# Five input tiles in flight, the first two convolutions cut by token group, the norm row spread by TensorE, and the first prefix recurrence moved from slot 2 to slot 3: one change to a hybrid decoder layer

## The chip, the cores and the metric

The kernel runs on the 8 cores of one Trainium2 chip. The time is the device time of the slowest core in microseconds (us). Where it matters, ratios are given to the kernel before that ran on the same chip in the same rounds. Some executions fall into a second, slower state, in which the cores of one die show a lower granted TensorE clock (one run of the kernel before took 2349.65 us); those are left out everywhere.

Engines are named as the profile names them: PE is TensorE (PEld its weight loads), DVE VectorE, ACT ScalarE, POOL GpSimd, SP SyncE.

## The reference

One step of a hybrid decoder layer, for four prompts of 2048 tokens and 128 sample sequences of 8 tokens. Cut to what the change touches:

```python
D_MODEL = 2048; C_A = C_B = 1024; CONF_KW = 31; LRU_KW = 4; D_FF = 6144

def mixer(xn, conf_buf, lru_buf, h0, p, reset_first):
    proj = xn @ p['w_in']
    a_val, a_gate, b_x, b_gate = jnp.split(proj, [C_A, 2 * C_A, 2 * C_A + C_B], axis=-1)
    u = a_val * jax.nn.sigmoid(a_gate)
    ca, new_conf = causal_dwconv(u, conf_buf, p['conf_dw_w'], p['conf_dw_b'])      # 31 taps
    ca = jax.nn.silu(layer_norm(ca, p['conf_ln_g'], p['conf_ln_b']))
    xc, new_lru = causal_dwconv(b_x, lru_buf, p['lru_conv_w'], p['lru_conv_b'])    # 4 taps
    h, h_last = rglru(xc, h0, ...)      # two 128x128 gate products per head, sigmoids, a scan over time
    cb = h.astype(xn.dtype) * jax.nn.gelu(b_gate)
    return jnp.concatenate([ca, cb], axis=-1) @ p['w_out'], new_conf, new_lru, h_last

# layer:  x + norm(mixer(norm(x)));  then  x + norm(conv_ffn(norm(x)))   -- the larger part of the time
```

A core takes half of one prompt's tokens (1184 "active" columns with its samples) and, because the recurrence runs over time, a prefix of 992 columns for which only the recurrence is computed. That makes 17 tiles of 128 tokens. Tiles 0 to 9 in loading order carry the active columns, tiles 10 to 16 the rest of the prefix.

## The kernel before

The program is written once as a list of operations with the buffers that each reads and writes. Each engine executes its own operations in exactly the order in which they stand in the program; semaphores are derived from the buffers. So where a line stands decides what it queues behind on its engine. `mm` goes to PE, `act` to ACT, `tt`, `ts`, `stt` and `dcopy` to DVE.

A tile is loaded, normed (a square with sum on ACT, a 128x2048 scaling on DVE) and turned (16 transposes on PE into two PSUM banks, each evacuated by one copy on DVE or ACT):

```python
def p0_load(n):
    i, sl = xorder[n], n % 3                                # three tile buffers
    load("sp", r_x, T[f"xt{sl}"][:], xall[128 * i:128 * i + 128, :], [], [(f"xt{sl}",)])

def p0_norm(n):
    ...
    act(xs[:], xt[:], AF.Square, [kx], [ks, ("tiny", sl, 0)], accum=c[:, 0:1])
    act(c[:, 1:2], c[:, 0:1], AF.Ln, ...)
    act(c[:, 2:3], c[:, 1:2], AF.Exp, ...)
    stt(xs[:], xt[:], c[:, 2:3], T["grow0"][:], ALU.mult, ALU.mult, [kx, ("tiny", sl, 2), "grow0"], [ks])

def p0_turn(n):
    for kh in range(2):
        ...                                                 # 8 transposes of 128x128 into bank 6 + kh
        eng = "act" if kh == 1 and n % 2 == 0 else "dve"
        evac(eng, ...)                                      # PSUM -> xna (active) or xnp (prefix)
```

The first stage projects channel groups 0 and 1 for five groups of tokens, while the tiles come in. `conv_diag(j)` builds the 31 diagonal matrices with which a depthwise convolution runs on PE; it is one DVE instruction.

```python
p0_load(0)
setup_first()            # vectors, flags, identity; the norm row broadcast by DMA to 128 partitions
p0_load(1)
load_w(2, after=[("xt0",)])
p0_load(2)
load_w(4, after=[("xt2",)])
conv_diag(0)
p0_norm(0)
G5 = [(0, 160), (160, 416), (416, 672), (672, 928), (928, NACT)]
def early(g):            # gate and value projection of channel groups 0 and 1, one token group
    ...
p0_norm(1); setup_second(); conv_diag(1); conv_load(0); conv_load(1)
for g in range(5):
    n = 2 * g
    p0_load(n + 3); p0_turn(n)
    p0_load(n + 4); p0_turn(n + 1)
    p0_norm(n + 2)
    if g < 4: p0_norm(n + 3)
    early(g)
...
b = conv(0, range(5), turn_more)    # turn_more: one of the tiles 10 to 16 between the pieces
conv_out(0, b)
b = conv(1, range(5), turn_more)
P_bx(0)                             # prefix projection of recurrence 0
conv_out(1, b); P_evac(0); P_conv(0)
```

After that come slots 2 to 7, each with one channel group of the convolution module and parts of one recurrence:

```python
for j in range(2, 8):
    i = j - 1
    ...
    proj(bg, "g", j, ACT3);  act(T["th"][:], ..., AF.Sigmoid, ...)
    if j == 2: P_gate(0, "wab"); P_sig(0, "p1", V_BA)
    else:      P_gate(i - 1, "wxb"); P_sig(i - 1, "p3", V_BX); P_in(i - 1); P_mult(i - 1)
    proj(bv, "v", j, ACT3);  uout(j, ...)
    if j == 2: P_gate(0, "wxb"); P_sig(0, "p3", V_BX); P_in(0); P_mult(0)
    P_scan(i - 1)                   # DVE scan over time
    P_bx(i)                         # prefix projection (PE)
    P_evac(i)                       # PSUM -> SBUF (ACT)
    P_conv(i)                       # four-tap convolution and cast to bf16 (DVE)
    bc = conv(j, [0])
    P_gate(i, "wab")
    conv_out(j, bc)
    P_sig(i, "p1", V_BA)
```

Of the kernel before, what the change touches and what calls it, by code (L numbers as in the profile page):

```python
# [55 lines left out]
class Sched:  # L56
# [135 lines left out]
    "hm23": 0, "gbg2": 0, "xna1": 4640, "x2_0": 0, "ca1": 0, "xnp1": 23584, "dstg": 2304, "ca2": 39456, "wp3": 8448,  # L192
    "t1_1": 23584, "wp7": 12544, "A3": 44096, "xcpZ": 48736, "diag0": 48736, "xs2_1": 16640, "xn21": 20736, "hstf":
    52704, "wo00": 39200, "catA5": 47392, "diag1": 56672, "xnp0": 64608, "hm3": 16640, "hm4": 39200, "t2_0": 28512,
    "wu2": 80480, "wo10": 8192, "xna0": 84576, "xn20": 49728, "wo13": 68192, "grow3": 18944, "t2_1": 33440, "wu4":
    103520, "xs1": 39456, "wu1": 107616, "ca4": 111712, "ca6": 116352, "ca7": 120992, "hm11": 41504, "ca5": 125632,
    "catB6": 76384, "f34": 2304, "ge1": 43808, "xc1": 53248, "wo01": 125632, "og0": 68192, "grow1": 78720, "bxp":
    130272, "ov0": 72928, "f31": 27136, "ca0": 134272, "catA7": 103520, "p3Z": 53248, "hm1": 77664, "hm14": 79968,
    "hm12": 82272, "t3_1": 58176, "hm13": 84576, "grow2": 86912, "x2_1": 95104, "t3_0": 63104, "wu3": 138912,
    "wo02": 105856, "hP": 143008, "bxe": 68032, "catA4": 133824, "ssf": 33280, "fl": 33568, "wo12": 114048, "grow0":  # L200
    111712, "rs": 72992, "hm7": 86880, "wp11": 103296, "t1_0": 143040, "f30": 43808, "f36": 49952, "wp5": 107392,
    "ubf1": 143040, "wab": 147968, "xsh": 122240, "hm0": 89184, "catA2": 136160, "wxb": 150016, "ov1": 111488,
    "us1": 146368, "cv": 152064, "vecs": 152192, "ge0": 116224, "hm5": 91488, "hm6": 93792, "xcb1": 49728, "flags":
    155072, "tiny": 155104, "gh": 138496, "xcb0": 77632, "dj": 37664, "btl": 155360, "f37": 56096, "bxpZ": 57216,
    "hm18": 96096, "p1Z": 143040, "ffo": 120992, "f32": 62240, "xs2": 119904, "hh1": 68384, "catB7": 123264,
    "identb": 155456, "catB3": 155712, "catA0": 158048, "ht": 143040, "gbg1": 160384, "ffp": 48576, "hm17": 98400,
    "slruc": 165024, "slruh": 166560, "xcp": 155712, "wp4": 133280, "f33": 111488, "xt1": 124000, "xcpbZ": 61216,
    "xs2_0": 165024, "hh0": 117632, "wo11": 169120, "wp1": 160384, "hm15": 100704, "hm20": 137376, "sq": 159680,
    "f38": 125824, "catA1": 177312, "wo03": 179648, "hm21": 139680, "catB2": 187840, "hm10": 141984, "lrucf":
    190176, "xc0": 167072, "wp6": 155712, "gbg0": 191808, "hm19": 144288, "wu0": 172000, "xt2": 176096, "hm22":  # L210
    146592, "hm16": 148896, "catB0": 196448, "p1": 176096, "hh2": 164480, "A3b": 184288, "ve1": 169120, "f35":
    172672, "wp8": 178816, "p3": 180064, "us0": 147008, "th": 167072, "mu": 179648, "catB4": 198784, "catA6":
    201120, "wu5": 198784, "hm9": 182912, "catB5": 203456, "ubf0": 188928, "hm2": 185216, "wp0": 190176, "hm8":
    187520, "xh": 205792, "prv": 194272, "zh": 194272, "xs0": 192256, "wp2": 200416, "wp9": 204512, "ve0": 173888,
    "ones": 164416, "ca3": 202880, "xcpb": 192256, "catB1": 207840, "catA3": 210176, "wp10": 208608, "xt0": 202880,
    "og1": 194272,
# [3 lines left out]
def build_program():  # L220
# [36 lines left out]
    with ExitStack() as es:  # L257
# [17 lines left out]
            ("grow0", [D], F_, 0, 2), ("wab", [8, 128], B_, 1, 18), ("wxb", [8, 128], B_, 1, 18),  # L275
            ("slruc", [8, 16, 3], F_, 1, 18), ("slruh", [8, 16], F_, 1, 18),
# [4 lines left out]
            ("bxp", [3 + NPRE], F_, 2, 9), ("xcp", [NPRE], F_, 2, 9), ("xcpb", [NPRE], B_, 2, 9),  # L281
            ("p1", [NPRE], F_, 2, 9), ("p3", [NPRE], F_, 2, 9),
# [13 lines left out]
        for i in range(3):  # L296
            BUFS += [(f"gbg{i}", [NCAT], F_, (9.5, 10, 11)[i], (18, 18.4, 17)[i])]
            BUFS += [(f"xt{i}", [D], F_, 0, 2), (f"xs{i}", [D], B_, 0, 2)]
            BUFS += [(f"hh{i}", [D], F_, 22.9, 24)]
# [17 lines left out]
        for i in range(8):  # L317
            BUFS += [(f"ca{i}", [NCAT], F_, max(1, i), (11, 13, 15, 17)[i // 2])]
# [82 lines left out]
        seq += [("g", 0), ("v", 0), ("g", 1), ("v", 1), ("x", 0)]  # L401
        for j in range(2, 8):
            seq += [("g", j), ("v", j), ("x", j - 1)]
# [25 lines left out]
        def setup_first():  # L429
            load("sp", r_su, vecs[:], vecs_d, [], ["vecs"])  # L430
            load("sp", r_su, flags[:], flags_d, [], ["flags"])
            load("pool", r_su, identb[:], ident_d, [], ["identb"])
            load("sp", r_su, T["grow0"][:], grows_d[0:1, :].partition_broadcast(128), [], ["grow0"])

        def setup_second():
            act(cv[:, 0:8], vecs[:, V_LAM:V_LAM + 8], AF.Exp, ["vecs"], [("cv", "e")], scale=-1.0)
            act(cv[:, 0:8], cv[:, 0:8], AF.Ln, [("cv", "e")], [("cv", "l")], bias=1.0)
            ts(cv[:, 8:16], cv[:, 0:8], -4.0, None, ALU.mult, None, [("cv", "l")], [("cv", "h")])
            ts(cv[:, 0:8], cv[:, 0:8], -8.0, None, ALU.mult, None, [("cv", "l")], [("cv", "f")])
            ts(cv[:, 16:32], vecs[:, V_BA:V_BA + 16], 0.5, None, ALU.mult, None, ["vecs"], [("cv", "b")])  # L440
            memset(ones[:], 1.0, [], ["ones"])
# [4 lines left out]
        def p0_load(n):  # L446
            i, sl = xorder[n], n % 3
            load("sp", r_x, T[f"xt{sl}"][:], xall[128 * i:128 * i + 128, :], [], [(f"xt{sl}",)])

        def p0_norm(n):  # L450
            sl = n % 3
            xt, xs, kx, ks = T[f"xt{sl}"], T[f"xs{sl}"], (f"xt{sl}",), (f"xs{sl}",)
# [4 lines left out]
            stt(xs[:], xt[:], c[:, 2:3], T["grow0"][:], ALU.mult, ALU.mult, [kx, ("tiny", sl, 2), "grow0"], [ks])  # L457

        def p0_turn(n):
            i, sl = xorder[n], n % 3  # L460
            xs, ks = T[f"xs{sl}"], (f"xs{sl}",)
            for kh in range(2):
# [9 lines left out]
                eng = "act" if kh == 1 and n % 2 == 0 else "dve"  # L472
# [55 lines left out]
        def conv(j, tags, between=None):  # L528
# [4 lines left out]
            for g in range(4):  # L533
# [8 lines left out]
                if between is not None:  # L542
                    between(g)
            return b0

        def conv_out(j, b0):
# [5 lines left out]
            kk = [(kc, 0), (kc, 1)]  # L552
            if j == 0:
                dcopy(T["A3b"][:], ca[:], kk, ["A3b"])
                act(T["A3"][:], ca[:], AF.Square, kk, ["A3"])
            else:
                sq = T["sq"][:, 0:NCAT]
                act(sq, ca[:], AF.Square, kk, ["sq"] + [("sq", g) for g in range(5)])
                tt(T["A3b"][:], T["A3b"][:], ca[:], ALU.add, kk + ["A3b"], ["A3b"])
                tt(T["A3"][:], T["A3"][:], sq, ALU.add, ["sq", "A3"], ["A3"])  # L560
# [17 lines left out]
        def pb(j, name):  # L578
            return name + ("Z" if j == 7 else "")

        def P_evac(j, b0=6):
            nb = pb(j, "bxp")
            bxp = T[nb]
            if j == 0 or j == 7:
# [178 lines left out]


        p0_load(0)
        setup_first()
        p0_load(1)
        load_w(2, after=[("xt0",)])
        p0_load(2)
        load_w(4, after=[("xt2",)])  # L770
        conv_diag(0)
        p0_norm(0)
        G5 = [(0, 160), (160, 416), (416, 672), (672, 928), (928, NACT)]
        stb = {"b": 0}

        def early(g):
            a0, a1 = G5[g]
            n = a1 - a0
            for j in range(2):
                gt, kg = (T["th"], ("th", g)) if j == 0 else (T["sq"], ("sq", g))  # L780
                bs = []
                for kind in "gv":
                    b = stb["b"] % 6
                    stb["b"] += 1
# [6 lines left out]
                act(gt[:, a0:a1], pg, AF.Exp, PK(bs[0]), [kg], scale=-1.0)  # L791
                act(gt[:, a0:a1], gt[:, a0:a1], AF.Ln, [kg], [kg], bias=1.0)
                act(gt[:, a0:a1], gt[:, a0:a1], AF.Exp, [kg], [kg], scale=-1.0)
                uout(j, pv, gt[:, a0:a1], PK(bs[1]) + [kg], a0, a1, g)

        p0_norm(1)
        setup_second()
        conv_diag(1)
        conv_load(0)
        conv_load(1)  # L800
        for g in range(5):
            n = 2 * g
            p0_load(n + 3)
            p0_turn(n)
            p0_load(n + 4)
            p0_turn(n + 1)
            p0_norm(n + 2)
            if g < 4:
                p0_norm(n + 3)
            early(g)  # L810
        done_w("v", 1)

        nx = {"n": 10}

        def turn_more(g):
            n = nx["n"]
            if n >= 17:
                return
            if n + 3 < 17:
                p0_load(n + 3)  # L820
            if n + 1 < 17:
                p0_norm(n + 1)
            p0_turn(n)
            nx["n"] += 1

        trip["n"] = 0
        b = conv(0, range(5), turn_more)
        conv_out(0, b)
        b = conv(1, range(5), turn_more)
        P_bx(0)  # L830
        conv_out(1, b)
# [4 lines left out]

        for j in range(2, 8):
            conv_load(j)
            i = j - 1
# [560 lines left out]
```

## Time and profile before

| | before |
|---|---|
| median | 1879.52 us (1877.62, 1879.52 and 1879.96) |
| profiled execution, slowest core (3) | 1875.9 us |
| first transposes / first projection / second token group start | 17.65 / 32.62 / 49.50 us |
| convolution 2 ends | 186.2 us |
| gate product after convolution 4 | 263.84 us |
| first output-projection matmul, cores 0 to 7 | 552, 558, 549, 559, 556, 548, 557, 549 us |

The page of the profile of before, its top, its rows of PE and of PE's granted clock in 40 slices of 47 us, and the summary of the chain of waits:

```profile
span 1875.9 us, 33549 instructions; the slowest of 8 cores (1863.6 to 1875.9 us)
...
PE 1757.1 (94%) x10400; PEld 913.3 (49%) x10400; DVE 988.9 (53%) x994; ACT 564.0 (30%) x1007; POOL 126.9 (7%) x239
...
PE   2889999989987999999999999999999999999993
...
PEclk9999999989988999999999999999999999999997
...
PE 85%; DMA 8%; ACT 2%; DVE 2%; issue 2%; SPq 0%; POOL 0%; DVEq 0%; ACTq 0%; POOLq 0%
```

PE is busy 94% of the time and 85% of the chain is PE itself. What an off-path engine does is free here, except where PE waits for it. The first digit of the PE row is a 2: in the first 47 us PE works two tenths of the time. That slice is the change's target.

The timeline of core 3 before (start in us, length, engine, line, operation, out<-in, shape, count, and in brackets the idle time before it with what ended it):

```profile
10.84 4.29 DVE L359 TENSOR_TENSOR sb_diag_102<-sb_identb,sb_vecs 128x3968 bf16<-128x3968 bf16 x1 [10.84 <-DMA sb_identb<-ident]
15.05 2.34 DVE L368 SCALAR_TENSOR_TENSOR sb_xs_92<-sb_xt_91,sb_tiny,sb_grow_51 128x2048 bf16<-128x2048 f32 x1
17.65 1.87 PE L467 MATMUL ps<-sb_identb,sb_xs_92 128*128 128x128 bf16 x16 [17.65 <-DVE sb_xs_92 L368]
...
26.84 0.53 POOL L377 DMA_DIRECT2D sb_wu_187<-w_in  x1 [17.31 <-DMA sb_xt_99<-xall]
...
32.62 1.22 PE L374 MATMUL ps<-sb_xna_130,sb_wu_185 128*128 128x160 bf16 x8
...
40.76 1.23 PE L374 MATMUL ps<-sb_xna_130,sb_wu_187 128*128 128x160 bf16 x8 [3.92 <-DMA sb_wu_187<-w_in]
...
49.50 1.03 PE L374 MATMUL ps<-sb_xna_130,sb_wu_185 128*128 128x256 bf16 x8 [0.19 <-DVE sb_xna_130 L347]
...
186.19 0.58 PE L374 MATMUL ps<-sb_xcpb,sb_wab 128*128 128x496 bf16 x2
...
263.84 0.58 PE L374 MATMUL ps<-sb_xcpb,sb_wab 128*128 128x496 bf16 x2
```

The first tile had landed at 8.0 us, but DVE was building the diagonals of convolution 0 (4.29 us at 10.84), and the tile's scaling stood behind it. The third weight was issued only at 26.84 us, and PE waited 3.92 us for it at 40.76.

The waits of PE on that core in the first 200 us, by releaser (total us, number of waits, longest):

```profile
PE ps L467 <- DVE sb_xs_92 L368: 17.6, 1, 17.6
PE ps L467 <- DVE sb_xna_130 L347: 17.4, 5, 11.2
PE ps L467 <- DVE sb_xnp_131 L347: 5.3, 1, 5.3
PE ps L374 <- DMA sb_wu_187<-w_in: 3.9, 1, 3.9
```

The transposes of a tile wait for the evacuation of the tile before, because both use PSUM banks 6 and 7.

### The profile page before, as it was taken

The page shows a single profiled execution, that of the slowest core. Times are in us where ns is not written, and L with a number is a line of the kernel's source. Part 1 is how long each engine was busy: PE and PEld are TensorE (multiplying, and loading weights), DVE is VectorE, ACT ScalarE, POOL GpSimd, SP SyncE. Part 2 cuts the span into 40 slices and gives each one's busy share as a digit, 9 for nine tenths or more (in the row PEclk, how much of TensorE's full clock was granted, in tenths as well). Part 3 has the DMA queues.
Part 4 walks back from the last instruction along what each step waited for, and adds up shares of the span by engine and source line. Part 5 has one row for each costly group of instructions (what it writes and reads, how often), then busy time and mean ns, then how long its engine had stood idle before and what let it go on. Part 6 is the DMA issues. An engine that isn't in the chain of part 4 may idle for free.

```text
span 1875.9 us, 33549 instructions; the slowest of 8 cores (1863.6 to 1875.9 us)
## 1 busy us (share of the span) xinstructions
PE 1757.1 (94%) x10400; PEld 913.3 (49%) x10400; DVE 988.9 (53%) x994; ACT 564.0 (30%) x1007; POOL 126.9 (7%) x239
## 2 busy tenths in 40 slices
PE   2889999989987999999999999999999999999993
PEld 2765555544442444555555544444555555544441
DVE  4544545547884565666666640002666666652243
ACT  2642343257883443222222211111222222211121
POOL 1000000001120001000000000001000000000000
PEclk9999999989988999999999999999999999999997
DMA  8653233222258547744444325556444444355756
GB/s 202 204 129 64 45 81 53 50 35 46 46 99 206 171 153 158 135 69 68 68 69 68 68 63 118 118 118 124 68 68 69 68 69 69 68 138 116 187 195 199
DMA packets 54259, 194.25 MB, mean 104 GB/s; under 512 B 7232, under 2 KB 10944, under 8 KB 46656
## 3 DMA queue, kind: packets, MB, share of 16 engines
q0 software_dynamic: 29232, 106.41, 33.7%
q1 hardware_dynamic: 24848, 85.69, 13.5%
q8 instruction: 84, 1.38, 0.3%
q14 instruction: 95, 0.78, 0.1%
HBM read 267.56 MB, written 32.35 MB: 160 GB/s over the span
## 4 chain that ended last, share of the span: by engine, by line
PE 85%; DMA 8%; ACT 2%; DVE 2%; issue 2%; SPq 0%; POOL 0%; DVEq 0%; ACTq 0%; POOLq 0%
PE ps L374 85%; DMA sb_xt_99<-xall 2%; DMA sb_wo_206<-w_out 1%; DMA sb_prv<-f_scr 1%; DMA sb_xt_95<-xall 1%; DMA y<-sb_hh_101 1%; DMA sb_wu_187<-w_in 1%; DMA y<-sb_hh_97 1%; ACT L341 0%; PE ps L467 0%; PE ps L1043 0%; DMA sb_wab<-wa 0%; SPq L377 0%; DVE sb_fl L359 0%; DVE sb_ht L368 0%
## 5 line engine op out<-in xcount | busy, mean ns | idle before, releaser
L347 DVE COPY sb_ve_113<-ps 128x1026 f32<-128x1026 f32 (+1 forms) x48 | 36.4, 800 | 297.8 <-PE ps L374 297.8
L347 DVE COPY sb_ve_127<-ps 128x1026 f32<-128x1026 f32 (+1 forms) x48 | 36.4, 800 | 114.1 <-PE ps L374 114.1
L368 DVE SCALAR_TENSOR_TENSOR sb_ov_129<-sb_ve_127,sb_vecs,sb_ov_129 128x1184 f32<-128x1184 f32 x48 | 69.7, 1451 | 5.3 <-DVE sb_ov_129 L368 0.5
L368 DVE SCALAR_TENSOR_TENSOR sb_og_128<-sb_ge_126,sb_vecs,sb_og_128 128x1184 f32<-128x1184 f32 x48 | 69.7, 1452 | 5.0
L368 DVE SCALAR_TENSOR_TENSOR sb_og_114<-sb_ge_112,sb_vecs,sb_og_114 128x1184 f32<-128x1184 f32 x48 | 69.7, 1451 | 5.0
L368 DVE SCALAR_TENSOR_TENSOR sb_ov_115<-sb_ve_113,sb_vecs,sb_ov_115 128x1184 f32<-128x1184 f32 x48 | 69.6, 1451 | 5.0
L339 ACT COPY sb_dstg<-ps 128x512 f32<-128x512 f32 x36 | 20.9, 587 | 159.6 <-PE ps L374 159.6
L374 PE MATMUL ps<-sb_ubf_117,sb_diag_116 128*128 128x342 bf16 (+1 forms) x496 | 64.1, 291 | 0.0
L374 PE MATMUL ps<-sb_ubf_103,sb_diag_102 128*128 128x342 bf16 (+1 forms) x496 | 62.2, 286 | 0.0
L339 ACT COPY sb_ffo<-sb_ve_127 128x32 f32<-128x32 f32 x24 | 5.3, 219 | 182.6 <-DVE sb_ve_127 L347 182.6
L339 ACT COPY sb_ffo<-sb_ve_113 128x32 f32<-128x32 f32 x24 | 5.3, 220 | 175.5 <-DVE sb_ve_113 L347 175.5
L341 ACT ACTIVATE sb_og_128<-sb_og_128 128x1184 f32<-128x1184 f32 x24 | 28.6, 1191 | 83.0 <-DVE sb_og_128 L368 83.0
L374 PEld LDWEIGHTS ps<-sb_ubf_117,sb_diag_116 128*128 128x128 bf16 x496 | 43.9, 99 | 19.7
L341 ACT ACT_TABLE_LOAD x37 | 47.5, 1283 | 17.9 <-PE ps L374 7.0
L341 ACT ACTIVATE sb_og_114<-sb_og_114 128x1184 f32<-128x1184 f32 x24 | 28.6, 1192 | 79.3 <-DVE sb_og_114 L368 79.3
L374 PEld LDWEIGHTS ps<-sb_ubf_103,sb_diag_102 128*128 128x128 bf16 x496 | 43.2, 97 | 18.5
L339 ACT COPY sb_ge_112<-ps 128x1026 f32<-128x1026 f32 (+1 forms) x48 | 31.4, 706 | 33.6 <-PE ps L374 33.6
L339 ACT COPY sb_ge_126<-ps 128x1026 f32<-128x1026 f32 (+1 forms) x48 | 31.4, 706 | 27.4 <-PE ps L374 27.4
L374 PE MATMUL ps<-sb_xna_130,sb_wu_187 128*128 128x512 bf16 (+2 forms) x184 | 34.2, 333 | 3.9 <-DMA sb_wu_187<-w_in 3.9
L374 PE MATMUL ps<-sb_xn_132,sb_wp_207 128*128 128x512 bf16 (+1 forms) x192 | 35.1, 325 | 0.5 <-DVE sb_xn_132 L347 0.5
L374 PE MATMUL ps<-sb_xn_132,sb_wp_209 128*128 128x512 bf16 (+1 forms) x192 | 35.1, 325 | 0.3 <-ACT sb_ge_112 L339 0.3
L374 PE MATMUL ps<-sb_xn_135,sb_wp_207 128*128 128x512 bf16 (+1 forms) x192 | 35.1, 325 | 0.1
(671 smaller groups left out, 4067.5 us busy)
## 6 DMA issues: line engine op xcount, KB each, us to landing
f_scr<-sb_dstg SPq DMA_DIRECT2D x36, 256.0 KB, 3.5
sb_prv<-f_scr SPq DMA_DIRECT2D x36, 256.0 KB, 5.6
sb_xt_91<-xall SPq DMA_DIRECT2D x6, 1024.0 KB, 6.8
sb_xt_95<-xall SPq DMA_DIRECT2D x6, 1024.0 KB, 10.4
sb_xt_99<-xall SPq DMA_DIRECT2D x5, 1024.0 KB, 11.3
sb_x_0_110<-xall SPq DMA_DIRECT2D x5, 1024.0 KB, 6.7
h_scr<-sb_x_0_110 SPq DMA_DIRECT2D x5, 1024.0 KB, 3.8
sb_x_1_124<-xall SPq DMA_DIRECT2D x4, 1024.0 KB, 5.2
```

What stands on the lines that cost most here:

```text
L339: S.op("act", lambda e: e.copy(out=out, in_=in_), reads, writes)
L341: S.op("act", lambda e: e.activation(out=out, in_=in_, func=func, scale=scale, bias=bias), reads, writes)
L347: S.op("dve", lambda e: e.tensor_copy(out, in_), reads, writes)
L368: S.op("dve", lambda e: e.scalar_tensor_tensor(out, a, s, b, op0, op1), reads, writes)
L374: S.op("pe", lambda e: e.matmul(out, lhsT, rhs, start=start, stop=stop, skip_group_check=skip), reads, writes)
```

## The change

Its intent: get the first stage off the ground sooner, and have PE work ready while tiles arrive.

1. Five tile buffers at first instead of three, and all four weights queued as soon as tile 0 has landed.
2. The norm row comes as one row of 8 KB and is spread over the partitions by four one-row matmuls and four copies, instead of a broadcast DMA. Half of the vector table loads later.
3. The diagonal builds move behind the first two token groups, and tile norms and turns move between the projections of a group.
4. Convolutions 0 and 1 run per token group (`early_conv`), and projection 2 and convolution 2 run before the first prefix projection.
5. Recurrence 0 starts in slot 3 instead of slot 2's first gate; slot 3 now holds two recurrences, with a second set of buffers ("Y").

The diff, without the new table of buffer addresses and the smaller edits:

```diff
 def p0_load(n):
-    i, sl = xorder[n], n % 3
+    i, sl = xorder[n], xslot(n)             # n % 5 for the first ten tiles
 def p0_norm(n):
     ...
     stt(xs[:], xt[:], c[:, 2:3], T["grow0"][:], ALU.mult, ALU.mult, ...)
+    if n + XD(n) < 17:
+        p0_load(n + XD(n))
 def p0_turn(n):
-    eng = "act" if kh == 1 and n % 2 == 0 else "dve"
+    eng = "act" if kh == 1 and (n % 2 == 0 or n < 4) else "dve"
 ...
+load("sp", r_su, T["grow0"][0:1, :], grows_d[0:1, :], [], [("grow0r", c) for c in range(4)])
+p0_load(0)
+...
+load_w(4, after=[("xt0",)])
+for n in range(1, 5):
+    p0_load(n)
+for c in range(4):
+    mm(PS[:, 512 * c:512 * c + 512], ones[0:1, :], T["grow0"][0:1, 512 * c:512 * c + 512], True, True, ...)
+for c in range(4):
+    dcopy(T["grow0"][:, 512 * c:512 * c + 512], PS[:, 512 * c:512 * c + 512], ...)
+p0_norm(0); setup_second(); p0_norm(1); conv_load(0); conv_load(1)
+def next_tile(n):
+    if n < 17:
+        p0_turn(n)
+    if n + 2 < 17:
+        p0_norm(n + 2)
+next_tile(0)
+next_tile(1)
 for g in range(5):
-    ...
-    early(g)
+    early(g, lambda j: next_tile(2 * g + 2 + j))    # after the projections of channel group j
+    if g < 2:
+        conv_diag(g)
+    if g >= 2:
+        early_conv(g - 2)
+    ...
+# projection 2 (gate), early_conv(3, [0]), projection 2 (value), early_conv(3, [1]), conv(2), tiles 12 to 16 between
+P_bx(0)
 ...
-for j in range(2, 8):
+for j in range(3, 8):
+    if j == 3:
+        P_bx(1, bx1); P_evac(1, bx1)
     proj(bg, "g", j, ACT3)
     A_gate(j, bg)
+    if j in (3, 4):
+        P_gate(j - 3 + (j == 4), "wab"); P_sig(j - 3 + (j == 4), "p1", V_BA)
+        if j == 3: P_conv(1)
     ...
     proj(bv, "v", j, ACT3)
     uout(j, ...)
+    if j in (3, 4):
+        h = 0 if j == 3 else 2
+        P_gate(h, "wxb"); P_sig(h, "p3", V_BX); P_in(h); P_mult(h); P_scan(h)
+    if j == 3:
+        P_gate(1, "wab"); P_sig(1, "p1", V_BA)
+        bc = conv(j, [0])
+        P_gate(1, "wxb"); P_sig(1, "p3", V_BX)
+        conv_out(j, bc)
+        P_in(1); P_mult(1)
+        P_bx(2)
+        P_evac(2)
+        P_scan(1)
+        P_conv(2)
+        continue
```

## The prediction

> **What bounds the kernel now.** PE is busy 94% of 1875.9 us; the chain of waits is 85% PE. The change touches only the first 190 us. The slice table shows PE at 2 tenths in the first 47 us. The timeline of the slowest core (3):
> - first tile landed at 8.0 us, but its scaling stood behind a 4.3 us diagonal build on DVE; first transposes 17.6 us;
> - tile 0's evacuation stood behind the norm of tile 1 (landed 20.3 us); first projection 32.6 us;
> - projections j=1 waited for weights (40.6, 43.9 us) issued only at 26.8 us, because three tiles, two weights and a 1 MB broadcast of the norm row filled the DMA until 26.3 us;
> - second token group 49.5 us; then waits of 4.8 and 5.3 us for tiles near 57 and 110 us, and 1.3 us each for gate weights (153 us) and a sigmoid (163 us);
> - convolution 2 ended at 186.2 us.
>
> Warm durations: 256-column group 7.0 us, convolution 15.3, tile transpose 0.89, prefix projection 6.7. All PE work up to 186.2 us is 32 + 3x15.3 + 17x0.89 + 2x6.7 + 16 + 1 = about 124 us, so 62 us are lost there.
>
> **What changes.**
> - The broadcast becomes an 8 KB row, four one-row matmuls and four copies, hidden under the first tile's load; half the vector table goes later. About 1.2 MB of early DMA vanish: 4-5 us at the 250-290 GB/s of mixed loads.
> - Five tiles and four weights queue at once; the idle DMA at 26-29 us (windows: 0.00) goes.
> - The diagonal build (4.3 us) and a table load (1.28 us) leave the first tile's path.
> - Convolutions 0 and 1 go per token group, and projection 2 and convolution 2 ahead of the first prefix projection, so PE has work while tiles 10-16 arrive. Matmul columns do not change.
> - New SBUF layout: I found no buffer whose predecessor is freed later in a way that matters; two output-weight loads should go 1 us earlier.
>
> **Estimate.** The first stage stays DMA-bound: 5 tiles, 4 weights and state, about 9.5 MB. Tiles beside weights came at 6.85 us per MB: tiles 1-3 at about 15, 21, 28 us; weights at 132 GB/s from 8.5 us: the last at about 40 us. First projection about 27 us, second token group 43-44 us instead of 49.5. From there PE is nearly always fed: 115 us of work plus 3 us of handoffs ends at about 161 us; the same work (without three gate products) ends at 185 us before. Gain 24 us. Slot 3 now holds two recurrences: 1.5 us lost behind a sigmoid (1.3 us seen at 163 us). Output weights +1. Net 23.5 us; the later stages, PE-bound, keep it.
>
> **Prediction: 1856 us, 8 in 10 between 1844 and 1867.** Faster by over 2%: 0.07; within 2%: 0.92; slower: 0.01.
>
> **The Trainium skill.** "TensorE: Matmul & The Clock Gate", part 1, says that the array runs at half rate after an idle window of about 3.4 us. The trace agrees: 16 transposes took 1.87 us after idle, 1.06 warm. About 2 us of the gain is clock, inside the figure.
>
> **What would show it.** First transposes near 14 us; second group near 43 us; no PE wait over 2 us between 45 and 160 us; prefix projection 1 ends near 161 us; from slot 4 on, every stage as long as before, shifted by 23 us.
>
> **What would make it wrong.** Weights served much later beside five queued tiles (gain 15); PE waiting on ACT in the early groups, since each gate stands behind the norm of a tile that may not have landed; PE stalls in slots 3-4 where recurrences pile up; output weights arriving no earlier, so part of the gain is waited away near 560-600 us.

## The result and the profile after

The median was 1871.47 us (1870.89 to 1873.81), against a median of 1879.52 us for before. The ratio is 0.9962 (95% interval 0.9943 to 0.9982), which counts as the same at the 2% threshold. It is above the predicted range of 1844 to 1867. A ratio here is the record's own figure, from the fast runs of the same rounds, so it is not quite the ratio of the medians.

The page after, the same lines:

```profile
span 1869.5 us, 33611 instructions; the slowest of 8 cores (1861.7 to 1869.5 us)
...
PE 1751.6 (94%) x10302; PEld 916.9 (49%) x10470; DVE 988.8 (53%) x997; ACT 569.0 (30%) x1016; POOL 128.5 (7%) x239
...
PE   6899899989987999999999999999999999999992
...
PEclk9899999999997999999999999999999999999996
...
PE 84%; DMA 7%; DVE 3%; ACT 3%; issue 2%; SPq 0%; POOL 0%; DVEq 0%; ACTq 0%; POOLq 0%
```

The first slice went from 2 tenths to 6: the target was hit. But the second slice of the clock row (47 to 94 us) fell from 9 to 8, the fifth of the PE row (187 to 234 us) fell from 9 to 8 too, and the second of the PE row is still 8. So something new is lost in both places. DVE and ACT grew from 2% to 3% of the chain.

The timeline of core 4 (the slowest after) in the first stage:

```profile
14.25 1.87 PE L474 MATMUL ps<-sb_identb,sb_xs_97 128*128 128x128 bf16 x16 [4.11 <-DVE sb_cv L368]
...
24.78 1.23 PE L379 MATMUL ps<-sb_xna_137,sb_wu_192 128*128 128x160 bf16 x8 [3.87 <-DVE sb_xna_137 L352]
...
38.93 1.84 PE L379 MATMUL ps<-sb_xna_137,sb_wu_192 128*128 128x256 bf16 x8
...
43.23 1.06 PE L474 MATMUL ps<-sb_identb,sb_xs_102 128*128 128x128 bf16 x16
...
45.86 2.35 DVE L373 SCALAR_TENSOR_TENSOR sb_xs_107<-sb_xt_96,sb_tiny,sb_grow_51 128x2048 bf16<-128x2048 f32 x1 [7.08 <-ACT sb_tiny L346]
...
48.36 4.28 DVE L364 TENSOR_TENSOR sb_diag_109<-sb_identb,sb_vecs 128x3968 bf16<-128x3968 bf16 x1
...
52.56 0.69 DVE L352 COPY sb_xna_137<-ps 128x1024 bf16<-128x1024 bf16 x1
...
53.39 1.86 PE L474 MATMUL ps<-sb_identb,sb_xs_107 128*128 128x128 bf16 x16 [5.62 <-DVE sb_xna_137 L352]
...
56.58 1.87 PE L379 MATMUL ps<-sb_xna_137,sb_wu_192 128*128 128x256 bf16 x8 [1.33 <-DVE sb_xna_137 L352]
...
61.39 1.04 PE L379 MATMUL ps<-sb_xna_140,sb_wu_193 128*128 128x256 bf16 x8
...
165.45 1.84 PE L379 MATMUL ps<-sb_xnp_141,sb_wu_193 128*128 128x496 bf16 x8
```

The transposes of tile 4 were done at 44.3 us (43.23 + 1.06). The copy that frees their bank ran on DVE at 52.56, eight microseconds later. In between, DVE did the scaling of a tile (45.86) and then the same 4.28 us diagonal build that had been in the way at 10.84 before. PE waited 5.62 us for that copy. The Trainium skill, "Perfetto Trace Analysis", section "Tensor Engine Instruction (MATMUL, LD_WEIGHTS)", says that "ACT/DVE/GPSIMD are strict FIFO"; this trace agrees, since the 0.69 us copy, ready at 44.3, did not pass the 4.28 us build.

The wait costs twice. From 51 to 61 us the windows show PE's granted clock at 0.50, and eight matmuls of 256 columns took 1.87 us at 56.58; eight of the same shape took 1.04 us at 61.39. The Trainium skill, "TensorE: Matmul & The Clock Gate", "Part 1: The HAM clock gate", gives half rate after an idle window of about 3.4 us, and about as long a time of work before full rate returns. On the first, this stretch agrees: PE had stood still for 5.62 us. On the second, it depends on what counts as work: the 256-column matmuls ran at half rate for some 4.5 us (56.58 to about 61), but the transposes had begun at 53.39, almost 8 us before full rate returned.

The windows of core 4 after, two stretches (busy time and count per engine, then granted clock, DMA share and GB/s):

```profile
51.00:61.00 10.00, 6.28 (x37) 4.70 (x38) 10.00 (x9) 3.69 (x8) 1.06 (x2) 0.50 1.03 318
...
222.00:226.00 4.00, 3.61 (x11) 1.51 (x13) 4.00 (x1) 1.09 (x1) 0.00 (x0) 0.63 0.21 41
```

In the first of them DVE is busy 10.00 of 10.00 us, while PE is busy 6.28: DVE's queue has no gap there in which the copy could have come sooner, so its order has to change, or the copy has to go to another engine. ACT was busy for 3.69 of these 10 us; moving the copy there was not tested.

The second stretch is at the end of slot 3. The timeline of core 4 there:

```profile
211.94 0.97 ACT L344 COPY sb_bxpY<-ps 128x992 f32<-128x992 f32 x1
...
213.63 2.22 DVE L628 TENSOR_TENSOR_SCAN sb_bxp<-sb_p_67,sb_p_68 128x992 f32<-128x992 f32 x1
...
217.03 3.96 DVE L373 SCALAR_TENSOR_TENSOR sb_xcpY<-sb_bxpY,sb_vecs,sb_xcpY 128x992 f32<-128x992 f32 x3
...
221.23 0.68 DVE L352 CAST sb_xcpbY<-sb_xcpY 128x992 bf16<-128x992 f32 x1 [0.24 <-DVE sb_xcpY L373]
...
222.17 0.98 PE L379 MATMUL ps<-sb_xcpbY,sb_wab 128*128 128x496 bf16 x2 [4.23 <-DVE sb_xcpbY L352]
...
255.81 0.58 PE L379 MATMUL ps<-sb_xcpb,sb_wab 128*128 128x496 bf16 x2
```

The input of recurrence 2 was in SBUF at 212.9 us. Its four-tap convolution began only at 216.1 us, because recurrence 1's scan (213.63 to 215.85) stood ahead of it on DVE. PE wanted the result for a gate product that takes 0.58 us when warm, waited 4.23 us, and then ran at half clock.

The waits of PE on core 4 from 36 to 260 us, answering the list above:

```profile
PE ps L474 <- DVE sb_xna_137 L352: 5.6, 1, 5.6
PE ps L379 <- DVE sb_xcpbY L352: 4.2, 1, 4.2
PE ps L379 <- ACT sb_p3Y L346: 2.7, 2, 1.3
...
PE ps L379 <- ACT sb_p_68 L346: 1.3, 1, 1.3
```

So there are two suspects, in two places: the DVE queue near 53 us, and the queue of two recurrences in slots 3 and 4. A reading of two traces cannot weigh them, and it does not exclude others. The rivals were that five tiles beside four weights hold up the DMA and tile 5 simply comes late; that convolutions per token group bring nothing; and that the first stage's gain is lost later, for example at the output weights.

Some numbers already speak against the last rival. From the start of the up-projection to the last matmul every core takes the same 377.4 + 748.2 us before and after, within 0.9 us. From the first output-projection matmul, where the output weights are used, to the up-projection it takes 156.9 to 160.1 us before and 157.7 to 161.0 us after. The first output-projection matmul moved from 552, 558, 549, 559, 556, 548, 557, 549 us to 550, 546, 547, 549, 548, 546, 546, 549 us. Four cores of before (1, 3, 4, 6), one of each pair of neighbours, were 6 to 10 us behind the others, and they gained about 10 us; the other four gained about 1.6 us. The last of all cores to get there came 8.5 us earlier (558.6 to 550.1 us). The time is that of the slowest core, so the 8 us are mostly the laggards catching up. Why the two cores of a pair drift apart in the first stage before was not tested.

### The profile page after: what moved, and what is told of

Read it like the earlier page. It is cut to its first block, busy times and chain, and to the rows that moved or that the text cites. A ratio compares the mean times of both kernels' runs of the same rounds, so it can differ in the third digit from the quotient of the medians.

```text
span 1869.5 us, 33611 instructions; the slowest of 8 cores (1861.7 to 1869.5 us)
## 1 busy us (share of the span) xinstructions
PE 1751.6 (94%) x10302; PEld 916.9 (49%) x10470; DVE 988.8 (53%) x997; ACT 569.0 (30%) x1016; POOL 128.5 (7%) x239
## 3 DMA queue, kind: packets, MB, share of 16 engines
q8 instruction: 84, 1.38, 0.3%
## 4 chain that ended last, share of the span: by engine, by line
PE 84%; DMA 7%; DVE 3%; ACT 3%; issue 2%; SPq 0%; POOL 0%; DVEq 0%; ACTq 0%; POOLq 0%
PE ps L379 83%; DMA sb_wo_213<-w_out 1%; DMA sb_wu_195<-w_in 1%; DMA sb_prv<-f_scr 1%; DMA y<-sb_hh_108 1%; PE ps L474 1%; DMA sb_xt_101<-xall 1%; ACT L346 1%; DMA y<-sb_hh_104 0%; PE ps L1139 0%; DMA sb_xt_96<-xall 0%; DVE sb_fl L364 0%; DMA y<-sb_hh_99 0%; DVE sb_ht L373 0%; DVE sb_xc_126 L373 0%
## 5 line engine op out<-in xcount | busy, mean ns | idle before, releaser
L379 PE MATMUL ps<-sb_ubf_110,sb_diag_109 128*128 128x342 bf16 (+3 forms) x527 | 62.3, 279 | 0.7 <-ACT sb_ca_199 L346 0.7
L379 PE MATMUL ps<-sb_ubf_124,sb_diag_123 128*128 128x342 bf16 (+3 forms) x527 | 62.3, 279 | 0.0
L346 ACT ACT_TABLE_LOAD x38 | 48.8, 1283 | 26.4 <-PE ps L379 14.1
```

The costliest lines, as they stand in the source:

```text
L346: S.op("act", lambda e: e.activation(out=out, in_=in_, func=func, scale=scale, bias=bias), reads, writes)
L379: S.op("pe", lambda e: e.matmul(out, lhsT, rhs, start=start, stop=stop, skip_group_check=skip), reads, writes)
```

## The experiments

All kernels gave correct results. In every table "conv 2" is the start of convolution 2, as the mean over the eight cores of the profile: it measures the first stage. "Slots 3-4" is the time from the first gate product of slot 3 to the one after convolution 4 on core 4: it measures the slots. "Chip" only says which kernels ran side by side.

| kernel | chip | median us | ratio to before (95%) | conv 2 | slots 3-4 |
|---|---|---|---|---|---|
| after | own | 1871.47 | 0.9962 (0.9943 to 0.9982) | 136.7 | 80.7 |
| a_diag: build of convolution 0 earlier | A | 1868.93 | 0.9951 (0.9937 to 0.9965) | 134.2 | |
| b_slots: slot order mended | A | 1862.34 | 0.9916 (0.9901 to 0.9931) | 137.2 | 72.2 |
| c_both: a and b | A | 1858.71 | 0.9898 (0.9882 to 0.9913) | 134.0 | 72.2 |
| d1_bcast: c with the norm row by DMA | A | 1864.13 | 0.9927 (0.9913 to 0.9941) | 137.3 | |
| e1_free: c with an earlier reload of tile 5 | B | 1867.02 | 0.9925 (0.9912 to 0.9937) | 137.4 | |
| e2_half: e1 with two weights first | B | 1863.92 | 0.9909 (0.9896 to 0.9923) | 137.2 | |
| d2_three: e1 with three tile buffers | B | 1868.71 | 0.9934 (0.9920 to 0.9947) | 138.1 | |
| d3_convlate: c without convolutions per group | B | 1870.32 | 0.9941 (0.9927 to 0.9954) | 143.8 | |
| f_best: c with both builds early, scalings late | C | 1861.35 | 0.9894 (0.9855 to 0.9933) | 134.9 | |
| g_front: after with f's first stage | C | 1871.80 | 0.9964 (0.9916 to 1.0011) | 134.7 | |
| h_defer: after with late scalings only | C | 1877.19 | 0.9991 (0.9948 to 1.0034) | 140.5 | |
| i_swap: after, scan 1 behind convolution of 2 | C | 1865.86 | 0.9919 (0.9875 to 0.9963) | 136.7 | 76.3 |
| j_best: c with builds early, scalings late where needed | D | 1855.15 | 0.9868 (0.9853 to 0.9883) | 128.9 | 72.2 |
| k_front: after with j's first stage | D | 1865.72 | 0.9955 (0.9921 to 0.9989) | 129.0 | 81.7 |
| l_after: after again | D | 1871.65 | 0.9957 (0.9943 to 0.9972) | 136.7 | 82.2 |

All of these ratios count as "same" at the 2% threshold. Some runs that the record calls fast were partly disturbed. On chip C, two runs of before (1894 and 1896 us) had cores 2 and 3 at a clock of 0.96. They make all four ratios of that chip too low by almost 0.002, so its medians are the safer figure.

### One suspect each: a_diag, b_slots, c_both

a_diag moves one line: the build of convolution 0 comes right after the turn of tile 3, before the norm of tile 5 instead of behind it.

```diff
             if n < 17:
                 p0_turn(n)
+            if n == 3:
+                conv_diag(0)
             if n + 2 < 17:
                 p0_norm(n + 2)
-            if g < 2:
+            if g == 1:
                 conv_diag(g)
```

> The changed kernel with one move: the diagonal build for convolution 0 (4.28 us on DVE) goes before the norm of tile 5 instead of after the first token group. My theory: DVE idles there (38.8 to 45.9 us in the profile after), so the wait of 5.6 us (3.0 to 5.7 over the cores) for tile 4's evacuation near 53 us falls below 2 us, the projections after it run warm (about 2.7 us), and convolution 2 starts 6 to 8 us earlier; total 1863 to 1866 us against 1871.5. Rival: the late tile (tile 5 landed at 43.2 us, tile 6 at 46.9) is what holds PE; then the wait only changes its name and the total stays within 2 us of 1871.

The first stage became 2.5 us shorter (134.2 against 136.7), and the median lies 2.5 us below that of after, less than half of what was expected; the intervals of the two ratios overlap. The wait did not go. In the profile of c_both, which has the same first stage, core 4 shows what took the build's place:

```profile
50.19 2.35 DVE L373 SCALAR_TENSOR_TENSOR sb_xs<-sb_xt,sb_tiny,sb_grow 128x2048 bf16<-128x2048 f32 x1 [1.91 <-ACT sb_sq L346]
...
52.79 1.28 DVE L352 COPY sb_xna<-ps 128x1024 bf16<-128x1024 bf16 x2
...
53.62 6.08 PE L379 MATMUL ps<-sb_xna,sb_wu 128*128 128x256 bf16 x32 [4.13 <-DVE sb_xna L352]
```

The transposes of tile 5 were done at 49.5 us. Their evacuation waited on DVE behind the scaling of tile 6 (50.19 to 52.54), which nobody needed yet. PE waited 4.13 us, and 32 matmuls of 256 columns took 6.08 us, which take 3.65 us at full clock. So the theory "the build causes the wait" was too narrow. The queue order on DVE causes it, and the build was only the first thing in the way.

b_slots moves the gate products and the sigmoids of the slots into the middle of longer PE work, so that ACT and DVE have time for them:

```diff
             bv = triple()
-            proj(bv, "v", j, ACT3)
+            for n in range(3):
+                proj(bv, "v", j, ACT3, only=n)
+                if n == 0 and j in (3, 4):
+                    h = 0 if j == 3 else 2
+                    P_gate(h, "wxb")
+                    P_sig(h, "p3", V_BX)
 ...
             if j == 3:
-                P_gate(1, "wab"); P_sig(1, "p1", V_BA)
-                bc = conv(j, [0])
-                P_gate(1, "wxb"); P_sig(1, "p3", V_BX)
-                conv_out(j, bc)
-                P_in(1); P_mult(1)
-                P_bx(2); P_evac(2); P_scan(1); P_conv(2)
+                def inside(g):           # called after pieces 0 and 1 of the convolution
+                    if g == 0:
+                        P_gate(1, "wab"); P_sig(1, "p1", V_BA)
+                    elif g == 1:
+                        P_gate(1, "wxb"); P_sig(1, "p3", V_BX)
+                        P_in(1); P_mult(1); P_scan(1)
+                bc = conv(j, [0], inside)
+                conv_out(j, bc)
+                P_bx(2); P_evac(2); P_conv(2)
```

> The changed kernel with the recurrences of slots 3 and 4 laid out anew: head 1's two gate products and its multiplier and scan go inside convolution 3, the second gate product of heads 0 and 2 goes inside the value projection, and head 2's short convolution comes before nothing but the evacuation it needs. My theory: the waits of 1.33, 1.33, 4.23 and 1.33 us at 185, 203, 222 and 234 us and about 1.6 us of half clock after the longest go; convolution 4 starts 8 to 10 us earlier; total 1862 to 1864 us. Rival: ACT and DVE simply have too much work in those slots (two recurrences each), so the waits come back in slot 5 or before convolution 3, and the total stays above 1868 us.

All four waits of slots 3 and 4 went, and one of 1.58 us on another DVE product came. The slots took 72.2 us instead of 80.7, the first stage stayed as it was (137.2), and the median fell to 1862.34 us. So the slots are worth about 9 to 10 us by themselves.

> Both moves together. If the two losses are independent, the gains add: 1854 to 1858 us, which is the figure first predicted, and the start of convolution 4 at about 223 to 225 us on the slowest core against 240.6. If one chain of ACT and DVE work sets both, the gain is that of the larger move alone, about 1863 us.

c_both has both edits. It took 1858.71 us: a_diag's and b_slots' gains over after (2.5 and 9.1) predict 11.7 by addition, and 12.8 were measured, so the two places do not interfere. The total is just above the expected 1854 to 1858 us, because a_diag's part fell short (after itself had run on another chip; j_best, k_front and l_after below repeat the sum on one).

### The parts of the change itself: d1_bcast, d2_three, d3_convlate

d1_bcast is c_both with the norm row broadcast by DMA again, behind the flags, and without the matmuls and copies that spread it:

```diff
-        load("sp", r_su, T["grow0"][0:1, :], grows_d[0:1, :], [], [("grow0r", c) for c in range(4)])
+        load("sp", r_su, T["grow0"][:], grows_d[0:1, :].partition_broadcast(128), [], [("grow0", c) for c in range(4)])
-        for c in range(4):
-            mm(...)
-        for c in range(4):
-            dcopy(...)
```

> Both moves, but the norm row comes again as a 1 MB broadcast by DMA, after the first tile, instead of one row spread by TensorE. My theory: 1 MB more in the first 36 us, all of it ahead of the last of four weights, costs 3.5 to 5 us at the measured 250 to 290 GB/s, seen whole at the end: 1859 to 1862 us. Rival: the early stage is bound by ACT and DVE order and not by DMA; then within 1 us of c_both.

It took 5.4 us more than c_both on the same chip. The second token group started at 42 to 45 us instead of 38 to 39, and the first transposes at 14.8 to 16.8 us instead of 13.5 to 14.1. The spreading by TensorE is therefore worth about 5 us, in line with the estimate of 4 to 5 us for it in the prediction.

e1_free (below) has five tile buffers; d2_three is e1_free with three (a later group of weights waits for tile buffer 2 instead of 3):

```diff
         def XD(n):
-            return 5 if n < 8 else 3 if n >= 10 else 9
+            return 3
         def xslot(n):
-            return n % 5 if n < 10 else (n - 10) % 3
+            return n % 3
 ...
-        for n in range(1, 5):
+        for n in range(1, 3):
             p0_load(n)
```

> e1_free with three tile buffers in flight in the first stage, as in the kernel before, instead of five. Theory: the DMA queue is kept full by three tiles and four weights as well (tile 3 is issued when tile 0 has been scaled, at about 14 us), so five buffers bring little: within 2 us of e1_free. Rival: prefetch depth carries the gain of the early stage, then 4 us or more slower than e1_free.

It took 1868.71 against 1867.02 us; the intervals of the ratios overlap. Five tiles in flight bring about 2 us at most. The likely reason, not tested, is that the DMA is full anyway in that stretch (its share is 1.02 from 8 to 20 us after, and 1.01 before).

d3_convlate is c_both with the pieces of convolutions 0 and 1 collected after the last token group:

```diff
             early(g, lambda j: next_tile(2 * g + 2 + j))
-            if g >= 2:
-                early_conv(g - 2)
-            if g == 4:
-                next_tile(12)
             if g == 2:
                 load_w(6, after=[("xt3",)])
+        for c in range(3):
+            early_conv(c)
+        next_tile(12)
```

> c_both, but the first three parts of convolutions 0 and 1 come after the fifth token group and not after groups 2, 3 and 4. Theory: without them PE outruns ACT, which needs about 10 us for two norms, two gates and the evacuations of a group against 8.8 us on PE, so PE waits 1 to 2 us in each of groups 2 to 4; 2 to 5 us slower than c_both: 1861 to 1864. If the order of the convolutions brings nothing, within 1.5 us of 1858.7.

The loss was larger than expected: the median is 12 us above c_both, and the ratio 0.0043 higher, which is 8 us (c_both ran on another chip). In its profile, cores 4 and 5 ran at a lower clock (0.962 and 0.965 against 0.977 to 0.980), so the 143.8 us for convolution 2 are from the undisturbed cores. On the undisturbed core 1, waits of 3.5, 2.7 and 2.7 us stand before token groups 2, 3 and 4 (counted from 0), 9.0 us together, and the 32 matmuls after each take 5.32 us. The first of the three has its like in c_both; the other two are new. The convolutions per group are therefore a real gain: they give PE work exactly where the tiles make it wait.

### Is tile 5 late? e1_free and e2_half

The trace after shows that tile 5 was requested only at 36.04 us, though its buffer had been free since about 14 us. The weights were ordered "after tile 0 has landed" by registering them as readers of tile 0's buffer, and a reload of this buffer waits for all of its readers, so for the last weight. e1_free orders the weights by a key of their own; e2_half in addition keeps the first two weights on the old order:

```diff
-            load("sp", r_x, T[f"xt{sl}"][:], xall[128 * i:128 * i + 128, :], [], [(f"xt{sl}",)])
+            load("sp", r_x, T[f"xt{sl}"][:], xall[128 * i:128 * i + 128, :], [],
+                 [(f"xt{sl}",)] + (["first"] if n == 0 else []))
-        load_w(4, after=[("xt0",)])
+        load_w(4, after=["first"])                                        # e1_free
+        load_w(2, after=[("xt0",)]); load_w(4, after=["first"])           # e2_half instead
```

> c_both with one key changed: the four first weight loads wait for tile 0 through a key of its own and no longer count as readers of tile 0's buffer, so the load of tile 5 into that buffer need not wait for them to land (issued at 36.0 us in the profile after, though the buffer was free at 14). Theory: tile 5 is issued near 14 us and the wait of 4.1 us near 53 us ends or shrinks; but five to seven tiles now share the DMA with the weights, so the last weight lands at 40 to 43 us instead of 36 and the second token group starts 3 to 6 us later. Net within 3 us of c_both (1858.7). Rival: tile 5's lateness was not what held PE near 53 us, it was ACT's own work; then the wait stays and the total is 3 to 6 us worse.

> c_both, but only the first two of the four weight loads count as readers of tile 0's buffer, so tile 5 is issued when the second weight lands, at about 27 us instead of 36. Theory: the DMA has no hole at 36 to 38 us, tile 5 lands 4 to 6 us earlier (36 to 38 us), the last weight at most 2 us later, and the wait of 4.1 us near 53 us with its half-clock matmuls (about 2.4 us) goes: 1853 to 1856 us. Rival as for e1_free: no better than c_both, 1858 to 1860.

The rival fell. With tile 5 early (on core 4 of e1_free it landed at 38.0 us instead of 43.0), the wait near 56 us stayed: 3.15 us in e1_free and 3.14 us in e2_half, again for an evacuation behind the scaling of tile 6. The second token group started later, at 43 to 46 us in e1_free and 43 to 45 us in e2_half, because the extra tile took its share of the DMA and the last weights landed later: PE now waited 5.0 us (e1_free) and 5.3 us (e2_half) for them on core 4, against 2.1 us after. What e2_half was expected to mend it did not mend. The Trainium skill, "DMA: Bandwidth & Descriptors", "Queues, rings and completion order", says that each DMA engine goes round-robin between the queues that have work, packet by packet. These runs fit that: a tile asked for earlier (at 13.40 instead of 36.04 us) pushed back the weights of another queue. They do not show the packets themselves. The accidental dependence after is thus no fault to mend; it keeps the DMA free for the weights.

### Mending the first stage: f_best, g_front, h_defer

If the DVE order causes the waits, they should vanish when the evacuations go first. f_best is c_both with both builds early (after the turns of tiles 2 and 3) and with each norm split: ACT's part stays, the scaling on DVE comes one turn later, behind the evacuations.

```diff
+            if n in (2, 3):
+                conv_diag(n - 2)
+            if 5 <= n < 16:
+                p0_norm(n + 1, "s")                              # the scaling on DVE
             if n + 2 < 17:
-                p0_norm(n + 2)
+                p0_norm(n + 2, "a" if n >= 4 else "as")          # ACT's part
```

> c_both with DVE's order in the first stage mended further: both diagonal builds go into idle DVE time before the second token group, and from tile 6 on the scaling of a tile comes after the evacuation of the tile before it, not ahead of it. Theory: what held PE near 53 us in c_both (4.1 us) and e1_free (3.15 us) is the scaling of tile 6 (2.35 us) standing ahead of tile 5's evacuation on DVE, whenever tile 5 lands; so the wait falls to about 1.3 us or less, the half clock after it goes, convolution 2 starts at 127 to 131 us instead of 132 to 136, and the total is 1852 to 1856 us. Rival: ACT sets the pace there; then the wait moves to the transposes of tiles 6 or 7 and the total stays within 2 us of c_both.

The wait near 53 us went, and convolution 0 started at 55.95 us on core 4 against 67.5 us after. But the stage as a whole gained nothing over c_both (134.9 against 134.0), and the total missed the expected 1852 to 1856 us. The timeline of f_best, core 4, shows a new wait:

```profile
105.94 1.27 PE L379 MATMUL ps<-sb_xna,sb_wu 128*128 128x160 bf16 x16
...
109.46 1.05 PE L477 MATMUL ps<-sb_identb,sb_xs 128*128 128x128 bf16 x16 [2.25 <-DVE sb_xs L373]
...
110.35 5.25 PE L379 MATMUL ps<-sb_ubf,sb_diag 128*128 128x128 bf16 x62
```

The deferred scaling of that tile ran at 106.97 to 109.31 us, and PE was out of other work at 107.2. The same happened again at 126.75 us. Deferring a scaling is right where it would block, and wrong where PE is about to need it.

The clock adds a lesson. After 2.25 us of idle time and 16 transposes, 62 convolution matmuls took 5.25 us instead of 3.64. The Trainium skill, "TensorE: Matmul & The Clock Gate", "Part 4: PE-mode transpose", says that transposes do not count as PE-busy in the same way. No run here shows that, and no fixed limit comes out either. The same wait, with the same transposes after it, left the clock at 1.00 on core 4 of g_front (below):

```profile
110.30 1.05 PE L477 MATMUL ps<-sb_identb,sb_xs 128*128 128x128 bf16 x16 [2.25 <-DVE sb_xs L373]
...
111.19 3.64 PE L379 MATMUL ps<-sb_ubf,sb_diag 128*128 128x128 bf16 x62
```

Of the 16 such waits on the eight cores of f_best, 12 were followed by a clock of 0.50. A wait of this length thus may or may not cost half clock.

g_front has the first stage of f_best with the slots of after; h_defer has only the deferral, with the builds where after has them:

```diff
 g_front: f_best's edit of next_tile, without b_slots
 h_defer: the split norm alone, conv_diag(g) still after token groups 0 and 1
```

> The same mending of the first stage on the changed kernel, with its slots 3 and 4 left as they are. If the losses of the first stage and of the slots are independent, this is as much slower than f_best as a_diag is than c_both (10 us): 1862 to 1866 us, with the waits of 1.33, 1.33, 4.23 and 1.33 us in slots 3 and 4 unchanged.

> The changed kernel with only the scaling behind the evacuation from tile 6 on; the diagonal builds stay where they are. Theory: two things stand ahead of the evacuations on DVE in turn, the 4.28 us build after group 0 and the scaling; with one of them taken away the other still holds PE, so 2 to 4 us of the first stage come back: 1867 to 1870 us. If the scaling alone was the cause, it equals g_front.

Both missed. g_front took 1871.80 us, as after (on other chips), with the same two waits of 2.25 us. h_defer was the slowest of all (1877.19 us): the build still stood ahead of the evacuations (one wait of 6.3 us on core 4), and the late scalings added three more waits of up to 2.25 us.

### Inside the slots: i_swap

i_swap exchanges two lines, so that the convolution of recurrence 2 goes ahead of the scan of recurrence 1:

```diff
                 P_evac(2)
-                P_scan(1)
                 P_conv(2)
+                P_scan(1)
```

> The changed kernel with one swap in slot 3: head 2's short convolution before head 1's scan on DVE. Theory: the 4.23 us wait at 222 us has two parts, the multiply and the scan of head 1 ahead of the convolution on DVE (about 3 us) and ACT's evacuation of head 2 behind head 1's multiplier chain (the rest); so 1 to 1.5 us of it stay, and the three waits of 1.33 us stay: 3 to 4 us faster than the changed kernel, 1867 to 1869 us. If ACT alone sets it, the wait stays 4.2 us and the total 1871.

```profile
215.77 0.58 PE L379 MATMUL ps<-sb_xcpbY,sb_wab 128*128 128x496 bf16 x2 [1.18 <-DVE sb_bxp L376]
```

The wait of 4.23 us fell to 1.18 us (core 4 of i_swap), and the half clock behind it went. The slots took 76.3 us against 80.7, 82.2 and 81.7 us in three kernels with the order of after (after, l_after and k_front), so 4 to 6 us came from two lines. The three waits of 1.33 us behind sigmoids stayed, as nothing had moved them.

### The two mends together and apart: j_best, k_front, l_after

j_best limits the deferral to the tiles where the DVE queue is in the way. k_front has that first stage with the slots of after, and l_after is after unchanged, as a control on the same chip.

Against f_best:

```diff
-            if 5 <= n < 16:
+            if 5 <= n <= 8:
                 p0_norm(n + 1, "s")
             if n + 2 < 17:
-                p0_norm(n + 2, "a" if n >= 4 else "as")
+                p0_norm(n + 2, "a" if 4 <= n <= 7 else "as")
```

> f_best with the scaling behind the evacuation for tiles 6 to 9 only; later tiles are scaled at once again. Theory: the waits of 2.25 us at about 110 and 127 us go, with the half clock after them (1.6 us each), and the wait near 53 us stays away; convolution 2 starts at 125 to 129 us and the total is 1852 to 1855 us, 17 to 19 us faster than the changed kernel on this chip. Rival: the time is made up elsewhere and the total stays at 1859 or more.

> The same mended first stage on the changed kernel, slots 3 and 4 unchanged. Theory: slower than j_best by what the slots cost, 9 to 10 us: 1861 to 1865 us, and 8 to 10 us faster than l_after; the waits of 1.33, 1.33, 4.23 and 1.33 us stay in the slots.

> The changed kernel once more, unchanged, as the control of this chip: 1869 to 1873 us.

The page of j_best, then its timeline on core 4:

```profile
span 1853.3 us, 33784 instructions; the slowest of 8 cores (1845.0 to 1853.3 us)
```

```profile
48.38 1.05 PE L477 MATMUL ps<-sb_identb,sb_xs 128*128 128x128 bf16 x16 [1.24 <-DVE sb_xna L352]
...
49.09 1.29 DVE L352 COPY sb_xna<-ps 128x1024 bf16<-128x1024 bf16 x2 [0.53 <-PE ps L477]
...
49.93 3.65 PE L379 MATMUL ps<-sb_xna,sb_wu 128*128 128x256 bf16 x32 [0.50 <-DVE sb_xna L352]
...
238.52 0.58 PE L379 MATMUL ps<-sb_xcpb,sb_wab 128*128 128x496 bf16 x2
```

The evacuation now starts before its transposes have all ended, PE waits 0.50 us where c_both waited 4.13, and the 32 matmuls take 3.65 us instead of 6.08. The gate after convolution 4 comes at 238.52 us, against 255.81 after and 263.84 before.

On one chip: j_best 1855.15, k_front 1865.72, l_after 1871.65 us. The first stage is worth 5.9 us (l to k), the slots 10.6 us (k to j), together 16.5 us; 17 to 19 were expected. Inside the profile the same two sums are 7.7 to 7.8 us (136.7 to 129.0 or 128.9) and 9.5 us (81.7 to 72.2). Two of k_front's six runs were at 1880 to 1881 us with cores 4 and 5 at a clock of 0.97, though the record calls them fast. That is why its ratio is no lower than that of l_after. Cores 0 to 3 were undisturbed in all six: the slowest of them took 1863.1 us in the mean, against 1870.4 us in l_after, 7.3 us less, which agrees with the profile. j_best beats both kernels: 1.3% under before and 0.9% under after.

## Why the prediction was wrong

The prediction said 1856 us, a gain of 23.5 us; the gain was 8 us. The mechanism of the first stage was right. Two terms of its sum were wrong.

**Right.** The first transposes started at 14.25 us (predicted near 14) and the second token group at 38.93 us (predicted 43 to 44; a gain of 4.6 us more). These 4.6 us were luck: the request of tile 5 was held back by a dependence that nobody had planned, and without it (e1_free, on top of c_both) the group starts at 43 to 46 us. The spread norm row was worth about 5 us (predicted 4 to 5; d1_bcast). The later stages kept what reached them: from the gate after convolution 4 on, the next gate follows 8.43 us later before and after, and the up- and down-projection take 377.4 + 748.2 us in both. From that gate to the end of the span it is 1612.1 us before (1875.9 - 263.84) and 1613.7 us after. So the doubts about output weights and the buffer layout came to little: a gain of 1 us was predicted, a loss of 1.6 us is seen, and the tail after the last matmul alone varies from 31 to 35 us between cores.

**Wrong, first step: "From there PE is nearly always fed: 115 us of work plus 3 us of handoffs ends at about 161 us."** From the start of the second token group to the end of prefix projection 1 it took 128.4 us (38.93 to 167.29), where 117.5 us were predicted: 10.9 us more. The largest part is visible: the wait of 5.62 us near 53 us, one of 1.33 us behind it, and half clock until 61 us. j_best needs 119.4 us for the same stretch (39.1 to 158.5), so this estimate was nearly right for a kernel whose DVE queue is in order. So the reordering on DVE gives back 9.0 of the 10.9 us. The step failed because it summed PE work and took the feeding for granted. The prediction knew the diagonal build only as something that "leaves the first tile's path". It did not ask in front of what the build stands at its new place. It had named a possible wait of PE for ACT in the early groups; the queue that mattered was DVE's.

**Wrong, second step: "Slot 3 now holds two recurrences: 1.5 us lost behind a sigmoid."** From the end of prefix projection 1 to the gate after convolution 4 it took 88.5 us after (167.29 to 255.81). The same work before took 77.65 us (186.19 to 263.84), plus 0.84 us for two gate products that now lie in this stretch. So 10.0 us were lost, not 1.5. The waits are three times 1.33 us behind sigmoids, 4.23 us behind the scan, and half clock after it. b_slots takes 80.1 us for the stretch and j_best 80.0 us. Here the prediction had seen the cause, and listed "PE stalls in slots 3-4 where recurrences pile up" among what could make it wrong; the size of the term was off by 8.5 us.

The sum closes. Starting from 23.5 us: 4.6 us more at the second group, 10.9 us less to the end of prefix projection 1, 8.5 us less in the slots, 2.6 us less from there to the end, which gives 6.1 us. The two profiled spans differ by 6.4 us, the medians by 8.0 us.

**Shown, and only argued.** Shown by experiments: the slot order costs 9 to 11 us (b_slots, j_best against k_front); the DVE order in the first stage costs 6 to 8 us (k_front against l_after); tile 5's late request, the number of tile buffers and the convolutions per group are not the loss (each was tested on top of other edits). j_best with both mends lands at 1855 us. Not tested alone: the late half of the vector table, and projection 2 and convolution 2 ahead of the first prefix projection. Only argued: why one core of each pair was 6 to 10 us behind in the kernel before, and so why four cores gained 10 us and four 1.6 us.

## What to carry to other kernels

When work for one engine is reordered, the queues of its helpers are reordered too: at every new place of a long DVE or ACT instruction, ask which short one behind it frees something that the bound engine needs, and put the short one first. Defer preparation only where it blocks, since deferred to just before its use it makes a new wait; and count a wait of several microseconds on PE with the half clock after it, which made 32 matmuls of 3.65 us take 6.08. A sum of the bound engine's work is a lower limit, and two chains put into one slot need each handoff checked for the time that the helper engine needs for it.

## What the Trainium skill lacked or had wrong

- "TensorE: Matmul & The Clock Gate", Part 1: its idle window of about 3.4 us is not a safe limit here. On core 0 of the kernel after, PE stood still for 2.29 us before 486.40 us, with no transposes near, and the clock was 0.50 behind it (eight matmuls of 512 columns took 3.15 us instead of 1.89). A wait of 2.28 us before 524.69 us on the same core left the clock at 1.00.
- "ScalarE: Activation LUTs", "What ACT_TABLE_LOAD costs": it gives about 1.28 us for the load and about 1.38 us more for a drain. The load agrees, the drain is not seen. On core 4 after, an activation of 1.17 us starts at 204.28, the table load takes 1.28 us at 205.47, and the next activation starts at 206.76; the switch costs 1.3 us.
- Of this program and not of the chip, so no page has it: an order put on a load by naming a buffer as read also delays the reload of that buffer. Tile 5's request went out at 36.04 us for a buffer free at about 14 us, and releasing it earlier made the start of the second token group 4 to 8 us later, core by core (e1_free).
- No page says that two neighbouring cores can drift apart in one execution: before, cores 1, 3, 4 and 6 reached the output projection 6 to 10 us after their neighbours, and after at most 4.4 us lay between any two neighbours. The cause is open.
